# Hybrid attention/mLSTM layer on one core: the second feed-forward's gated tiles turned by VectorE and a trip through DRAM instead of TensorE, its down products taken by pairs of column blocks

## The chip, the core and the metric

The kernel runs on one core of a Trainium2 chip. A core has five engines that each work through a queue of their own, in order: PE (TensorE, matrix products), DVE (VectorE), ACT (ScalarE), POOL (GpSimd) and SP (SyncE, which here only issues transfers). They wait for each other by semaphores. Sixteen DMA engines move data between DRAM and the core's memory SBUF; a transfer is issued by SP, ACT or POOL and lands some time later. Products are summed in PSUM, used here as eight banks of 128 x 512 float32.

The metric is device time of one execution in microseconds, the median of several runs; lower is better.

## The reference

One layer of a diffusion backbone on 256 latent tokens and 256 context tokens of width 2048, all float32: a half-step SwiGLU feed-forward, a mixing stage (grouped-query attention beside a bidirectional mLSTM), and a second half-step SwiGLU feed-forward. The change is in the second feed-forward, which only the 256 latent tokens pass through:

```python
def half_step_ffn(x, mod, i, g, w_up, w_down):
    h = adaln(x, g, mod, i)
    a, b = jnp.split(h @ w_up, 2, axis=-1)
    return x + 0.5 * mod[:, i + 2, None, :] * ((jax.nn.silu(a) * b) @ w_down)
```

`D_FF` is 5632. A "gated tile" below is a piece of `silu(a) * b`: 128 tokens by 512 hidden columns.

## The kernel before, in words

**Products in three parts.** A float32 operand is split into a high part `hi` (rounded to the format float32r) and the rest `lo`. `split` (L120) does this for each half of a loaded weight tile of 128 x 2048: ACT writes `hi`, DVE writes `lo`, 128 x 1024 each, into rings of four buffers. `mm3` (L148) then issues three matmuls: high by high, and the two mixed ones. So for each megabyte of weights ACT and DVE make two passes each, and PE issues 12 matmuls (quads, below) or 24 (up and down steps).

**Hidden blocks.** The 5632 hidden columns are 11 blocks of 512, `n` = 0 to 10. Block 0 is made together with the end of the mixing stage, block 10 by plain up steps (`up`, L2180). Blocks 1 to 9 are made by `quad(n)` (L2078): the tokens are two halves `t` of 128, the 2048 inputs two halves, and seven products of combinations of those quarters (Strassen's scheme in Winograd's form) take the place of eight. Its seven products, `m` = 0 to 6, are two steps `s` each, one for each weight tile `q`. Their weights are sums of slices of `w_up2b`, made while they load: POOL's `accum` transfers (L740, a helper's line) add a slice to a buffer `chain` or `ra` that already holds one; SP loads the plain ones (`raw`, `ra`, `chain`). `summed_half` adds two buffers on DVE. At the end of `m` = 4 the gated tile of `t` = 0 exists (`c12`), at the end of `m` = 6 that of `t` = 1 (`c21`), each as 128 tokens (partitions) x 512 hidden columns, in a tile `ca`, with the sign reversed.

**Turning.** The down product needs the hidden columns on the partitions. `turned` (L2044) does it: four PE transposes of 128 x 128 into one PSUM bank (L2058), then ACT writes the high half `hid2h` from PSUM (L2061, which also mends the sign) and DVE the low half `hid2l` (L2063). It is called after every step; a tile is turned two steps after it was made (`N_TURN`). Block 10's two tiles (`sab`) go the same way.

**Down steps.** `down(n0, n1)` (L2213) multiplies two hidden blocks by their slices of `w_dn2`, for the four blocks of 512 output columns in turn: (n0, column 0), (n1, column 0), (n0, column 1) and so on, one step `u` each, a megabyte of `w_dn2` and 24 matmuls. After the second step of a column the two sums are added to `acc2` (L2229 on DVE, L2227 on ACT the first time). `units` strings the up steps of block 10 and down(0,1), (2,3), (4,5), (6,7); down(8,9) follows the last quad, and `last2` (L2278) does block 10 and the final norm.

**Order.** `sequence` (L2242) sets it: `s s` for each of the seven products, with a `u` after m = 1, 2, 4 and 5 (after all of 1 to 6 in the first quad). A scheduler then orders each engine's queue by its own estimate of times; only instructions marked `pinned` keep their order in the program. The first feed-forward already turns its tiles by the other way: `nc.vector.transpose` (L840), stores by SP to `hidd` (L842), loads by SP (`hid_load`, L705), and halves by `split_to` (L716, instructions at L720 and L721).

Of the kernel before, what the change touches and what calls it, by code (L numbers as in the profile page):

```python
# [37 lines left out]
N_TURN = 2  # L38
# [20 lines left out]
def tile_layer(ctx: ExitStack, tc: tile.TileContext, I: dict, out: bass.AP):  # L59
# [1871 lines left out]
    with f2x:  # L1931
# [111 lines left out]

        def turned():  # L2044

            if not turn:
                return
            n, t, sa, sign = turn[0]
            if clock[0] < born[n, t] + N_TURN:
                return  # L2050
            if n not in hids:
                if n - 1 not in hids or len(hids) - len(summed) >= N_HID:
                    return
                hids[n] = hid_tiles()
            turn.pop(0)
            tb = tbank()
            for j in range(FB):
                nc.tensor.transpose(tb[:, j * P : (j + 1) * P], sa[:, j * P : (j + 1) * P], ident)  # L2058
            t3 = tb.rearrange("p (j c) -> p j c", j=FB)
            hh, hl = (x[:, :, t * P : (t + 1) * P] for x in hids[n])  # L2060
            nc.scalar.activation(hh, t3, AF.Copy, scale=sign)  # L2061
            if sign < 0:
                nc.vector.scalar_tensor_tensor(hl, t3, -1.0, hh.bitcast(F32), op0=ALU.mult, op1=ALU.subtract)  # L2063
            else:
                nc.vector.tensor_tensor(hl, t3, hh.bitcast(F32), op=ALU.subtract)
            done.add((n, t))
# [3 lines left out]
        def wait_turn(n, t, sa, sign):  # L2070
            turn.append((n, t, sa, sign))
            born[n, t] = clock[0]
            turn.sort(key=lambda x: x[:2])

        def ca_tile():
            return f2b.tile([P, CB], F32, tag="ca", name="ca", bufs=3)

        def quad(n):  # L2078

            add = lambda o, x, y: nc.vector.tensor_tensor(o, x, y, op=ALU.add)  # L2080
            mul = lambda o, x, y: nc.vector.tensor_tensor(o, x, y, op=ALU.mult)
# [18 lines left out]
            def c12():  # L2100
                add(g["b"], B["X"], g["b"])
                mul(g["a"], g["a"], g["b"])
                wait_turn(n, 0, g["a"], -1.0)
# [76 lines left out]
        def up(n):  # L2180

            sab = []
            for ab in range(2):
                bs = [bank() for _ in range(2)]
                for u in range(4):
# [7 lines left out]
                    if u == 3:  # L2193
                        for t in range(2):
                            if ab:
                                nc.vector.tensor_tensor(sab[t], sab[t], bs[t], op=ALU.mult)
                                wait_turn(n, t, sab[t], 1.0)
# [15 lines left out]
        def down(*ns):  # L2213

            for cb in range(NCB):
                c = slice(cb * CB, (cb + 1) * CB)
                bs = [bank() for _ in range(2)]
                for n in ns:
                    assert (n, 1) in done or not n
                    wt = load_split(I["w_dn2"][n, cb])  # L2220
                    for t in range(2):
                        block(bs[t], n, wt, t, n == ns[0], n == ns[-1])
                    if n == ns[-1]:
                        for t in range(2):
                            a = acc2[:, t, c]
                            if not ns[0]:
                                nc.scalar.activation(a, bs[t], AF.Copy)  # L2227
                            else:
                                nc.vector.tensor_tensor(a, a, bs[t], op=ALU.add)  # L2229
                            if n == LAST - 1:  # L2230
                                half_gated(a, a, late["g8"][:, c])
                                accum(a, x2d[t * P : (t + 1) * P, c])
                        if cb == NCB - 1:
                            summed.update(ns)
                    yield
# [40 lines left out]
        drain(down(LAST - 2, LAST - 1))  # L2276
# [72 lines left out]
def _laid_out(a):  # L2349
# [30 lines left out]
    for n in "12":  # L2380
# [14 lines left out]
        rows = dn.reshape(NF // FB, FB, P, NCB, CB).transpose(0, 3, 2, 1, 4).reshape(NF // FB, NCB, P, 2048)  # L2395
        if n == "1":
            turned = dn.reshape(NF // FB, 4, FB, 32, NCB, CB).transpose(0, 4, 1, 3, 2, 5).reshape(NF // FB, NCB, P, 2048)
            rows = np.concatenate([rows[:1], turned[1:]])
        m[f"w_dn{n}"] = asc(rows)
# [34 lines left out]
```

## Time and profile before

| what | value |
|---|---|
| median of 3 runs | 2594.59 us (2590.64 to 2597.07) |
| the profiled execution | 2588.91 us, of which the span from the first to the last instruction is 2587.2 us |
| granted TensorE clock, mean | 0.995 |
| PE busy | 2555.3 us, 99% of the span |
| DVE busy | 2206.6 us, 85% |
| ACT busy | 1405.5 us, 54% |
| POOL busy | 221.9 us, 9% |
| moved by DMA | 684.70 MB, mean 265 GB/s |
| L2058, the transposes of `ca` | 72, first at 2000.3 us, last at 2514.6 us |
| weight transfers of a megabyte in the second feed-forward, issue to landing | medians 8.7 to 11.4 us |

In the rows, L152 is the line of `mm3`, so all products are there and are told apart by the tiles: `mm<-hi,hid2h` is a down step, `X<-` and `Y<-` are quads. L128 and L129 are the two instructions of `split`. Matmuls overlap each other in the pipeline: the time that one takes of PE is the distance between two starts, not its shown length. "DMA share" is the mean busy share of the sixteen engines.

### The profile page before, as it was taken

The page shows a single profiled execution, that of the slowest core. Times are in us where ns is not written, and L with a number is a line of the kernel's source. Part 1 is how long each engine was busy: PE and PEld are TensorE (multiplying, and loading weights), DVE is VectorE, ACT ScalarE, POOL GpSimd, SP SyncE. Part 2 cuts the span into 40 slices and gives each one's busy share as a digit, 9 for nine tenths or more (in the row PEclk, how much of TensorE's full clock was granted, in tenths as well). Part 3 has the DMA queues.
Part 4 walks back from the last instruction along what each step waited for, and adds up shares of the span by engine and source line. Part 5 has one row for each costly group of instructions (what it writes and reads, how often), then busy time and mean ns, then how long its engine had stood idle before and what let it go on. Part 6 is the DMA issues. An engine that isn't in the chain of part 4 may idle for free. (4 is left out here: it accounts for less than half of the span.)

```text
span 2587.2 us, 33868 instructions
## 1 busy us (share of the span) xinstructions
PE 2555.3 (99%) x12486; PEld 2124.7 (82%) x12486; DVE 2206.6 (85%) x2924; ACT 1405.5 (54%) x1798; POOL 221.9 (9%) x271
## 2 busy tenths in 40 slices
PE   8999999999999999999999999999999999999998
PEld 5788888888887878888889889888898888888886
DVE  7789888888888788888887888898889888898987
ACT  5454444444444455444454347466486676667763
POOL 0000000100010100010110000120000000000001
PEclk8999999999999999999999999999999999999999
DMA  9989999999999999999987897776768999999985
GB/s 392 355 214 275 265 290 277 262 292 281 276 285 282 255 236 246 213 221 231 231 242 268 295 315 242 237 282 212 267 233 246 275 277 283 278 286 278 273 248 171
DMA packets 153478, 684.70 MB, mean 265 GB/s; under 512 B 22872, under 2 KB 43864, under 8 KB 92000
## 3 DMA queue, kind: packets, MB, share of 16 engines
q1 hardware_dynamic: 123936, 490.64, 51.7%
q0 software_dynamic: 29376, 191.90, 37.3%
q8 instruction: 98, 1.61, 0.2%
q14 instruction: 68, 0.56, 0.1%
HBM read 664.59 MB, written 17.89 MB: 264 GB/s over the span
## 5 line engine op out<-in xcount | busy, mean ns | idle before, releaser
L128 ACT ACTIVATE hi<-raw 128x1024 fp32r<-128x1024 f32 (+2 forms) x488 | 504.5, 1040 | 401.2 <-PE mm L152 298.7
L129 DVE TENSOR_TENSOR lo<-raw,hi 128x1024 fp32r<-128x1024 f32 (+2 forms) x476 | 567.2, 1204 | 105.7 <-ACT hi L128 87.4
L128 ACT ACTIVATE hi<-chain 128x1024 fp32r<-128x1024 f32 x352 | 370.1, 1059 | 352.6 <-PE mm L152 199.3
L129 DVE TENSOR_TENSOR lo<-chain,hi 128x1024 fp32r<-128x1024 f32 x352 | 425.2, 1219 | 92.5 <-ACT hi L128 81.2
L152 PE MATMUL mm<-hi,hhi 128*128 128x512 f32 (+3 forms) x1024 | 390.7, 382 | 0.0
L152 PE MATMUL mm<-lo,hhi 128*128 128x512 f32 (+3 forms) x1024 | 387.7, 379 | 1.9 <-DVE lo L129 1.8
L152 PE MATMUL mm<-hi,hlo 128*128 128x512 f32 (+3 forms) x1024 | 386.6, 378 | 0.0
L208 DVE SCALAR_TENSOR_TENSOR junk<-sraw,cBh 128x1024 fp8e5<-128x1024 f32 x192 | 234.3, 1220 | 40.5 <-DMA sraw<-in_w_mt 39.0
L152 PEld LDWEIGHTS mm<-lo,hhi 128*128 128x128 f32 x1024 | 192.8, 188 | 37.0 <-DVE lo L129 4.0
L152 PEld LDWEIGHTS mm<-hi,hlo 128*128 128x128 f32 x1024 | 193.0, 189 | 32.0
L152 PEld LDWEIGHTS mm<-hi,hhi 128*128 128x128 f32 x1024 | 192.9, 188 | 32.2 <-ACT hi L128 0.3
L129 DVE TENSOR_TENSOR lo<-ra,hi 128x1024 fp32r<-128x1024 f32 x104 | 126.2, 1222 | 25.6 <-ACT hi L128 21.7
L128 ACT ACTIVATE hi<-ra 128x1024 fp32r<-128x1024 f32 x104 | 110.1, 1062 | 64.0 <-PE mm L152 34.2
L152 PE MATMUL mm<-lo,hid2h 128*128 128x512 f32 x352 | 137.1, 389 | 0.0
L152 PE MATMUL mm<-hi,hid2h 128*128 128x512 f32 x352 | 137.1, 389 | 0.0
L152 PE MATMUL mm<-hi,hid2l 128*128 128x512 f32 x352 | 137.0, 389 | 0.0
L152 PE MATMUL mm<-hi,sumshl 128*128 128x512 f32 x400 | 123.2, 389 | 0.0
L208 DVE SCALAR_TENSOR_TENSOR sr<-sr,cBl 128x1024 f32<-128x1024 f32 x84 | 102.1, 1222 | 16.4 <-DMA sr<-in_w_mt 15.1
L740 POOL DMA_DIRECT2D chain<-in_w_up1b x60 | 53.1, 886 | 724.1 <-DVE lo L129 583.9
L152 PE MATMUL mm<-hi,sumshh 128*128 128x512 f32 x352 | 108.3, 389 | 0.0
L152 PE MATMUL mm<-hhi,hi 128*128 128x512 f32 (+1 forms) x288 | 101.4, 352 | 0.0
L152 PE MATMUL mm<-hhi,lo 128*128 128x512 f32 (+1 forms) x288 | 99.0, 344 | 0.0
(490 smaller groups left out, 5415.1 us busy)
## 6 DMA issues: line engine op xcount, KB each, us to landing
raw<-in_w_dn SPq DMA_DIRECT2D x70, 1024.0 KB, 10.0
chain<-in_w_up1b POOLq DMA_DIRECT2D x60, 1024.0 KB, 10.7
sraw<-in_w_mt SPq DMA_DIRECT2D x96, 512.0 KB, 8.4
sr<-in_w_mt SPq DMA_DIRECT2D x81, 512.0 KB, 5.7
raw<-in_w_up1b SPq DMA_DIRECT2D x40, 1024.0 KB, 9.1
mraw<-in_w_m SPq DMA_DIRECT2D x32, 1024.0 KB, 7.6
chain<-in_w_dn POOLq DMA_DIRECT2D x30, 1024.0 KB, 10.2
chain<-in_w_up2b POOLq DMA_DIRECT2D x28, 1024.0 KB, 11.4
```

Of the source, the lines that this page charges most:

```text
L128: scalar[0].activation(hi, src, AF.Copy)
L129: vector[0].tensor_tensor(lo, src, hi.bitcast(F32), op=ALU.subtract)
L152: tensor[0].matmul(out_ap, s, m, start=first and not n, stop=last and n == 2, skip_group_check=skip)
L208: ins = nc.vector.scalar_tensor_tensor(junk() if junk else raw, raw, 1.0, cB[s], op0=ALU.mult, op1=ALU.mult, accum_out=mT[:, i, s, kt, h : ...
L740: accum = lambda dst, src: nc.gpsimd.dma_start(dst, src, accum_op=ALU.add)
```

## The change

- A quad's gated tile is now made with its right sign (`negative`, a scalar_tensor_tensor in place of a tensor_tensor). One step later DVE's transpose exchanges rows and columns inside each 32 x 32 square, from `ca` into the tile of the second factor (`spare`: `ca` or `cy`).
- At set places counted in steps, ACT's queue issues the rest: after 1 step (`N_STORE`) a store of the 128 x 512 tile to a DRAM tile `hid2`, after 4 and 5 steps (`N_FETCH`) two loads each of a band of 32 partitions, as 32 x 4 runs of 128 elements, and after 8 steps (`N_MOVE`) the high half (ACT) and low half (DVE), now from SBUF. All of these are pinned. A load waits for its tile's store to have landed.
- The rows of `w_dn2` for blocks 1 to 9 are laid out on the host in the order that this gives the hidden columns.
- Block 10's tiles still go through PE. The two PSUM banks of the transposes join the four for products.
- `down` takes column blocks in pairs: (n0, 0), (n0, 1), (n1, 0), (n1, 1), then the same for 2 and 3. At the end, the store and the loads of the last tile are placed around the first two steps of down(8,9), and block 10's transposes come after those.

```diff
-N_TURN = 2
+N_TURN = 1
+N_STORE = 1
+N_FETCH = 4
+N_MOVE = 8
...
-        ps["mm"] = ctx.enter_context(pool(name="ps2", bufs=4, space=PSUM))
+        ps["mm"] = ctx.enter_context(pool(name="ps2", bufs=6, space=PSUM))
         psx = ctx.enter_context(pool(name="psx", bufs=1, space=PSUM))
-        ps["tr"] = ctx.enter_context(pool(name="pt2", bufs=2, space=PSUM))
...
+        def halves(n, t, x, runs=False):
+            hh, hl = (y[:, :, t * P : (t + 1) * P] for y in hids[n])
+            if runs:
+                hh, hl = (y.rearrange("p j (a c) -> p a j c", c=32) for y in (hh, hl))
+            pinned(nc.scalar.activation(hh, x, AF.Copy))
+            pinned(nc.vector.tensor_tensor(hl, x, hh.bitcast(F32), op=ALU.subtract))
+            done.add((n, t))
+
         def turned():
...
-            tb = tbank()
-            for j in range(FB):
-                nc.tensor.transpose(tb[:, j * P : (j + 1) * P], sa[:, j * P : (j + 1) * P], ident)
-            t3 = tb.rearrange("p (j c) -> p j c", j=FB)
-            hh, hl = (x[:, :, t * P : (t + 1) * P] for x in hids[n])
-            nc.scalar.activation(hh, t3, AF.Copy, scale=sign)
-            if sign < 0:
-                nc.vector.scalar_tensor_tensor(hl, t3, -1.0, hh.bitcast(F32), op0=ALU.mult, op1=ALU.subtract)
...
+            if spare is not None:
+                turn.pop(0)
+                nc.vector.transpose(spare, sa)
+                moved.append((clock[0], n, t, sa, spare))
...
+        def stored(n, t, sa, spare):
+            pinned(nc.scalar.dma_start(hid2d[n][t], spare))
+
+        def fetched(n, t, sa, spare, bands):
+            rows = hid2d[n][t].rearrange("(a r) (b x) -> b r a x", a=4, b=4)
+            for b in bands:
+                pinned(nc.scalar.dma_start(sa[32 * b : 32 * b + 32].rearrange("r (a x) -> r a x", a=4), rows[b]))
+
+        def arrived():
+
+            for then, *x in moved:
+                age = clock[0] - then
+                if age == N_STORE:
+                    stored(*x)
+                elif age in (N_FETCH, N_FETCH + 1):
+                    b = 2 * (age - N_FETCH)
+                    fetched(*x, (b, b + 1))
+            if moved and clock[0] >= moved[0][0] + N_MOVE and room(moved[0][1]):
+                _, n, t, sa, _ = moved.pop(0)
+                halves(n, t, sa.rearrange("p (a j c) -> p a j c", a=4, j=FB), True)
...
-                mul(g["a"], g["a"], g["y"])
-                wait_turn(n, 1, g["a"], -1.0)
+                negative(g["a"], g["y"])
+                wait_turn(n, 1, g["a"], g["y"])
...
-            for cb in range(NCB):
-                c = slice(cb * CB, (cb + 1) * CB)
-                bs = [bank() for _ in range(2)]
+            for c0 in (0, 2):
+                bs = {}
                 for n in ns:
...
+                    for cb in (c0, c0 + 1):
...
-        while turn:
-            clock[0] += 1
-            turned()
-        before_final()
-        drain(down(LAST - 2, LAST - 1))
+        before_final()
+        final = down(LAST - 2, LAST - 1)
+        for gap, more in ((N_STORE, True), (N_FETCH - N_STORE, False), (1, True)):
+            clock[0] += gap
+            arrived()
+            if more:
+                next(final)
+        while moved:
+            clock[0] += N_MOVE
+            arrived()
+        while turn:
+            turned()
+        drain(final)
```

How the queues stand now. The first place is on ACT where quad 4 has ended and quad 5 runs its products m = 1 and m = 2 (`chain` and `ra` are the two pairs of weight buffers, `raw` the plain loads; `ca<-ca` is a silu, `ca<-X` a copy from PSUM). Before:

```order
L128 ACTIVATE hi<-raw 128x1024
L2112 ACTIVATE ca<-ca 128x512
L128 ACTIVATE hi<-raw 128x1024 x2
L2061 ACTIVATE hid2h<-tr 128x4x128
L128 ACTIVATE hi<-raw 128x1024
L2086 ACTIVATE ca<-X 128x512
L128 ACTIVATE hi<-raw 128x1024 x2
L128 ACTIVATE hi<-chain_15897 128x1024 x2
L2090 ACTIVATE ca<-ca 128x512
L128 ACTIVATE hi<-chain_15898 128x1024 x2
```

and with the change:

```order
L134 ACTIVATE hi<-raw 128x1024
L2151 ACTIVATE ca<-ca 128x512
L134 ACTIVATE hi<-raw 128x1024 x3
L2087 DMA hid_15907<-cy 128x512
L2125 ACTIVATE ca<-X 128x512
L2064 ACTIVATE hid2h<-ca 128x4x4x32
L134 ACTIVATE hi<-raw 128x1024 x2
L2092 DMA ca<-hid_15907 32x4x128 x2
L134 ACTIVATE hi<-chain_15894 128x1024
L2129 ACTIVATE ca<-ca 128x512
L2092 DMA ca<-hid_15907 32x4x128 x2
L134 ACTIVATE hi<-chain_15894 128x1024
```

Between the store (L2087) and the first pair of loads (L2092) ACT has a copy, the halves of the other tile and two weight passes; behind each pair stands a weight pass of product m = 2.

The second place is on DVE a little later, from the last pass over the first weight tile of m = 2 to the first `ra` tile of m = 3 (the rows `chain<-chain,ra` are `summed_half`; `raw` is m = 2's down step). Before:

```order
L129 TENSOR_TENSOR lo<-chain_15897,hi 128x1024
L2080 TENSOR_TENSOR chain_15897<-chain_15897,ra_15899 128x1024 x2
L129 TENSOR_TENSOR lo<-chain_15898,hi 128x1024
L2080 TENSOR_TENSOR chain_15898<-chain_15898,ra_15900 128x1024
L129 TENSOR_TENSOR lo<-chain_15898,hi 128x1024
L129 TENSOR_TENSOR lo<-raw,hi 128x1024 x2
L129 TENSOR_TENSOR lo<-ra_15899,hi 128x1024 x2
```

and with the change:

```order
L2119 TENSOR_TENSOR chain_15894<-chain_15894,ra_15896 128x1024
L135 TENSOR_TENSOR lo<-chain_15894,hi 128x1024
L135 TENSOR_TENSOR lo<-chain_15895,hi 128x1024 x2
L135 TENSOR_TENSOR lo<-raw,hi 128x1024 x2
L2065 TENSOR_TENSOR hid2l<-ca,hid2h 128x4x4x32
L2119 TENSOR_TENSOR chain_15894<-chain_15894,ra_15896 128x1024
L135 TENSOR_TENSOR lo<-ra_15896,hi 128x1024 x2
```

The addition that stood between the two passes over `chain_15898` stands elsewhere now; the two passes over the same tile, here `chain_15895`, follow each other.

The third place is the end on ACT with the change, after the silu of the last quad's last tile (here `raw` are tiles of `w_dn2`, and `hid2h<-mm` are block 10's halves):

```order
L134 ACTIVATE hi<-raw 128x1024 x4
L2151 ACTIVATE ca<-ca 128x512
L2087 DMA hid_15912<-cy 128x512
L134 ACTIVATE hi<-raw 128x1024 x2
L2092 DMA ca<-hid_15912 32x4x128 x2
L2064 ACTIVATE hid2h<-ca 128x4x4x32
L2092 DMA ca<-hid_15912 32x4x128 x2
L134 ACTIVATE hi<-raw 128x1024 x2
L2064 ACTIVATE hid2h<-ca 128x4x4x32
L2064 ACTIVATE hid2h<-mm 128x4x128 x2
```

Before, the last tile's four transposes stood on PE 15 matmuls into the down steps; now its halves (the second `hid2h<-ca`) come behind the store, both pairs of loads and four weight passes.

More of the change, by code (lines that the diff above doesn't have):

```diff
@@ L2042, in tile_layer, with room @@
         born, clock = {}, [0]
+        hid2d = {n: dr.tile([2, P, CB], F32, name=f"hid2{n}") for n in QUADS}
+        moved = []
+        def room(n):
+            if n not in hids:
+                if n - 1 not in hids or len(hids) - len(summed) >= N_HID:
+                    return False
+                hids[n] = hid_tiles()
+            return True
+        def halves(n, t, x, runs=False):
[5 more added lines that the diff above has]
+            done.add((n, t))
         def turned():
@@ L2059, in turned @@
-            t3 = tb.rearrange("p (j c) -> p j c", j=FB)
-            hh, hl = (x[:, :, t * P : (t + 1) * P] for x in hids[n])
-            nc.scalar.activation(hh, t3, AF.Copy, scale=sign)
-            if sign < 0:
[L2063 to L2066, printed above, removed]
+            if spare is not None:
+                turn.pop(0)
+                nc.vector.transpose(spare, sa)
+                moved.append((clock[0], n, t, sa, spare))
+            elif room(n):
+                turn.pop(0)
+                tb = bank()
+                for j in range(FB):
+                    nc.tensor.transpose(tb[:, j * P : (j + 1) * P], sa[:, j * P : (j + 1) * P], ident)
+                halves(n, t, tb.rearrange("p (j c) -> p j c", j=FB))
```

61 lines of the change are left out of this document (31 added, 30 removed).

## The prediction

> **What bounds the kernel now.** I read the busy time by stretches first, then the chain of waits, then the list of waits, all for the stretch from 2000 to 2500 us, in which the quads' tiles are turned (columns of the first: PE, weight load, DVE, ACT and POOL busy with their counts, granted clock, DMA share, GB/s).
>
> ```profile
> 2000.00:2100.00 100.00, 100.00 (x450) 82.66 (x449) 84.42 (x80) 69.87 (x76) 6.98 (x8) 1.00 0.96 292
> 2200.00:2300.00 100.00, 99.47 (x445) 81.81 (x444) 91.03 (x88) 69.29 (x74) 8.84 (x11) 1.00 0.92 274
> sum 500.00, PE 499.46 PEld 412.21 DVE 438.35 ACT 347.15 POOL 41.89; mean PE 99.89 PEld 82.44 DVE 87.67 ACT 69.43 POOL 8.38
> ```
>
> PE is busy for 499.5 of 500 us at full clock: it is the bound, and each PE instruction that goes is time that goes, as long as nothing else becomes late. The chain agrees (start, length, what):
>
> ```profile
> 2427.32 5.45 PE mm L152 x24
> 2432.76 0.44 PE tr L2058 x4
> 2433.20 5.45 PE X L152 x24
> ```
>
> The transposes are a link of it. But the cover is thin elsewhere (total us, times, longest):
>
> ```profile
> ACT hi L128 <- DMA chain<-in_w_up2b: 18.1, 7, 3.9
> ACT hi L128 <- DMA ra<-in_w_up2b: 9.7, 4, 2.8
> PE Y L152 <- DVE lo L129: 0.5, 1, 0.5
> ```
>
> Eleven times ACT waits for a weight that is still under way, up to 3.9 us; once this reaches PE. So DMA is not the bound on average, but there are places with almost nothing to spare.
>
> **What goes: PE.** The start times of PE's rows around one group of four transposes:
>
> ```profile
> 2504.18 0.39 PE L152 MATMUL mm<-lo,hid2h 128*128 128x512 f32 x1
> 2504.42 0.60 PE L2058 MATMUL tr<-ident,ca 128*128 128x128 f32 x4
> 2504.77 0.48 PE L152 MATMUL Y<-hi,h2hi 128*128 128x512 f32 x1
> 2505.09 0.40 PE L152 MATMUL Y<-hi,h2lo 128*128 128x512 f32 x1
> 2505.32 0.40 PE L152 MATMUL Y<-lo,h2hi 128*128 128x512 f32 x1
> ...
> L2058 PE MATMUL tr<-ident,ca x72: 270/272/304, 2000.3 to 2514.6; 128*128 128x128 f32 x72
> ```
>
> Products start every 0.23 us. From 2504.18 to 2505.09 two of them take 0.91 us, so the group costs 0.91 - 0.46 = 0.45 us, far less than four times its shown 0.27 us. 72 transposes are 18 groups: 18 x 0.45 = 8.1 us. Block 10's two groups stay.
>
> **What is added on DVE and ACT.**
>
> ```profile
> L840 DVE STREAM_TRANSPOSE c<-ca x20: 691/704/711, 208.3 to 922.5; 128x512 f32<-128x512 f32 x20
> L845 DVE SCALAR_TENSOR_TENSOR ca<-ca,cy x20: 679/684/693, 232.7 to 929.8; 128x512 f32<-128x512 f32 x20
> L2063 DVE SCALAR_TENSOR_TENSOR hid2l<-tr,hid2h x18: 683/684/694, 2002.6 to 2515.5; 128x512 fp32r<-128x512 f32 x18
> L721 DVE TENSOR_TENSOR sumshh<-hidl,sumshh x9: 1217/1219/1222, 944.3 to 1204.6; 128x1024 fp32r<-128x1024 f32 x9
> L842 SPq DMA_DIRECT2D hid<-c x20: 326/327/1792, 209.1 to 923.2; - x20
> L711 SPq DMA_DIRECT2D hidh<-hid x20: 325/480/704, 949.0 to 1229.8; - x20
> ```
>
> The first feed-forward shows the same instructions. The new one is the transpose, 0.70 us; the halves from SBUF in runs of 32 cost no more than those from PSUM (1.22 us for 1024 columns against 0.68 for 512), nor does the signed product (0.68 us; the plain product L2081 takes 0.68, in a row below). DVE gets 18 x 0.70 = 12.6 us into 500 - 438 = 62 idle ones: nothing, with PE as cover; were DVE the bound it would be 12.6 us. ACT gets five issues a tile, by SP's rows 0.33 + 4 x 0.48 = 2.3 us, 41 us into 153 idle ones: nothing as a sum. The danger is the order, because ACT's weight passes stand behind these issues.
>
> **ACT behind the store.** The first pair of loads waits until the store has landed, and product m = 2's weight passes wait behind it. Quad 4's second tile, from ACT's timeline and PE's (a pass of ACT is 1.06 us):
>
> ```profile
> 2211.02 1.06 ACT L128 ACTIVATE hi<-raw 128x1024 fp32r<-128x1024 f32 x1
> 2218.07 0.63 ACT L2090 ACTIVATE ca<-ca 128x512 f32<-128x512 f32 x1 [0.54 <-DVE ca L2080]
> 2222.41 2.01 ACT L128 ACTIVATE hi<-chain 128x1024 fp32r<-128x1024 f32 x2 [3.70 <-DMA chain<-in_w_up2b]
> 2221.95 0.62 PE L152 MATMUL Y<-hi,n1f 128*128 128x512 f32 x2
> ```
>
> The store can go at 2212.1 and lands L later. Behind it come a pair of loads (1.0), a pass (1.06), the silu (0.63), a pair (1.0), a pass (1.06) and its DVE pass (1.22): 6.0 us, so the second half of m = 2's first weight tile is ready at 2218.1 + L. PE starts m = 2 at 2221.95 and takes that low half as its ninth matmul, at 2223.8. An L up to 5.6 us costs nothing; beyond that each microsecond costs one, eight times over (quads 2 to 9 each follow such a tile). A first tile's store (t = 0) goes out one pass sooner, and its second pair stands behind both passes; by the same count it pays only from about 7.5 us. L has no row on ACT's queue, so I bound it:
>
> ```profile
> hid<-c SPq DMA_DIRECT2D x20, 256.0 KB, 7.4
> x2d<-x SPq DMA_DIRECT2D x8, 256.0 KB, 4.5
> out<-acc SPq DMA_DIRECT2D x8, 256.0 KB, 2.9
> ```
>
> These are stores of the same 256 KB: 2.9 us with the engines nearly free, 7.4 in the first feed-forward's full traffic, but behind megabyte loads in SP's own queue. ACT's queue holds nothing else, so I take 4.5 us: cost 0. At 7.4 it is 8 x 1.8 = 14 us.
>
> The Trainium skill ("DMA: Bandwidth & Descriptors", section "Anatomy of one DMA") gives a transfer about 2.0 us plus its bytes at 436 GB/s, by estimate 2.6 us for this store. The quiet row of 2.9 us agrees, the 7.4 us in traffic don't; by the rule this step costs 0 as well.
>
> **Weights that come later.** Per tile 0.26 MB are stored and 0.26 MB loaded on the same 16 engines.
>
> ```profile
> 2208.00:2212.00 4.00, 4.00 (x21) 3.15 (x20) 4.00 (x5) 3.58 (x5) 0.87 (x1) 1.00 0.97 205
> 2220.00:2224.00 4.00, 4.00 (x20) 3.30 (x19) 1.95 (x3) 1.59 (x2) 0.00 (x0) 1.00 1.01 418
> 2224.00:2228.00 4.00, 3.47 (x16) 2.56 (x15) 3.97 (x4) 3.26 (x4) 0.00 (x0) 1.00 0.37 156
> ...
> 2223.50 1.23 DVE L129 TENSOR_TENSOR lo<-chain,hi 128x1024 fp32r<-128x1024 f32 x1 [2.06 <-PE Y L152]
> 2224.76 1.22 DVE L2080 TENSOR_TENSOR chain<-chain,ra 128x1024 f32<-128x1024 f32 x1
> 2225.90 1.22 DVE L129 TENSOR_TENSOR lo<-chain,hi 128x1024 fp32r<-128x1024 f32 x1
> ```
>
> From 2208 to 2224 the engines are full, at 205 GB/s while accumulating and 418 with plain loads; then comes a gap (share 0.37). The waiting weight of 2222.41 lands at the end of the full stretch, and the store and first pair of a second tile (0.39 MB) now fall into it: 0.9 us later at 418 GB/s, 1.9 at 205. PE also arrives 0.45 us sooner. Against that, the addition between the two DVE passes (2224.76) now stands elsewhere, as the order rows show. It made the second pass end at 2227.1, and this is PE's one stall of 0.5 us, which goes. Without it the first pass decides: it ends at 2224.7, and PE, 12 matmuls after 2221.95, takes that low half as its third, at 2225.1. That is 0.4 us to spare, so a wait of about 3.7 + 0.4 = 4.1 us would be hidden. I apply that to all eleven places, of which these are the longest but the 3.70, and the shortest:
>
> ```profile
> 2012.30 2.01 ACT L128 ACTIVATE hi<-chain 128x1024 fp32r<-128x1024 f32 x2 [3.85 <-DMA chain<-in_w_up2b]
> 2465.96 2.01 ACT L128 ACTIVATE hi<-chain 128x1024 fp32r<-128x1024 f32 x2 [3.00 <-DMA chain<-in_w_up2b]
> 2283.09 2.01 ACT L128 ACTIVATE hi<-ra 128x1024 fp32r<-128x1024 f32 x2 [2.75 <-DMA ra<-in_w_up2b]
> 2137.07 1.06 ACT L128 ACTIVATE hi<-chain 128x1024 fp32r<-128x1024 f32 x1 [0.64 <-DMA chain<-in_w_up2b]
> ```
>
> At 0.9 + 0.45 = 1.35 us later only the waits of 3.85, 3.70 and 3.00 run over: 1.1 + 0.95 + 0.25 = 2.3 us. At 1.9 + 0.45 = 2.35 whatever exceeds 1.75 does, which is all but the shortest: 27.8 - 0.64 - 10 x 1.75 = 9.7 us. The new traffic is plain, so I take 2.3.
>
> **The end.** The last tile has only two down steps as cover.
>
> ```profile
> 2511.01 3.40 PE mm L152 x15
> 2513.41 0.68 DVE L2081 TENSOR_TENSOR ca<-ca,cy 128x512 f32<-128x512 f32 x1
> ```
>
> It is gated at 2514.1 and transposed at 2514.8. With L = 4.5 the first pair goes out by 2520.3, the other tile's halves and the second pair by 2521.9; the loads land 4.5 us later at 2526.4, and the high half is there at 2527.0. PE's two steps (10.9 us from 2511.0), block 10's transposes (0.9) and the first tile's 12 matmuls (2.7) end at 2525.5: 1.5 us of stall. With 2.9 us for both transfers it is 0; with L = 7.4 it is 4.4.
>
> **Sum.** -8.1 - 0.5 + 0 + 2.3 + 1.5 = -4.8 us. The profiled execution took 2588.9 us (span 2587.2, and 1.7 around it), so it would take 2584.1. The median of the runs shown lies 5.7 above the profiled execution: 2589.8.
>
> **Rivals.**
> - *Nothing comes late.* The stores land in 2.9 us and the gaps take the traffic: -8.6 us, 2586.0. For it: the first feed-forward does the same at a DMA share near 1. Against: its steps are twice as long, and SP, not ACT, waits there.
> - *ACT stands behind the store* (slower). L is 7.4 us as for `hid<-c`: -8.6 + 14 + 2.3 + 4.4 = +12.1, 2606.7. It decides from L = 5.6 on, cancels the gain at 6.1 us and passes it from there. For it: the same shape in the same traffic took 7.4. Against: that was behind SP's own loads. The Trainium skill (same page, "Issuing engines are not separate DMA queues") says that transfers of all issuers interleave on the same engines and a second issuer saves issue time alone; by this rule ACT's queue would help little, and the time is this rival's. No row of ACT's queue can tell.
> - *The weights come later by the slow rate.* -8.6 + 9.7 + 1.5 = +2.6: 2597.2. For it: the waiting weights are the accumulated ones, and their stretch begins at 205 GB/s. Against: what is added takes the engines' time by the plain rate.
>
> **How the numbers follow.** Forecast 0.40, nothing late 0.25, ACT behind the store 0.20, late weights 0.15. 0.3%, about what a measurement of this kernel can tell from no change, is 7.8 us: faster means below 2586.8. Most of "nothing late" lies there and a little of the forecast: 0.27. Slower means above 2602.4: ACT behind the store for the most part and the tail of late weights: 0.21. Within: 0.52. The forecast's own range is 2586 to 2594; with the others, 2584 (nothing late, and 2 us of scatter) to 2606.
>
> **What would show it.** No L2058 groups on `ca`, and 24 matmuls in 5.45 us without a gap: the gain. The store's median landing below or above 5.6 us, and ACT waiting for `hid` by name: which of forecast and second rival. Waits of ACT for `chain` and `ra` grown from 27.8 us in total, with PE rows released by `lo`: late weights. DVE above 95% in a stretch, or PE stalls where none of the three stands, would make the prediction wrong.

## The result and the profile after

The changed kernel takes 2669.81 us, median of 4 runs (2667.53 to 2672.66), against 2593.30 us of the kernel before in runs beside it (2590.64 to 2597.07): 76.5 us more, a ratio of 1.030 (95% interval 1.0285 to 1.0315). The prediction was 2589.8 us with a range of 2584 to 2606. It was wrong in size and in sign. The profiled execution took 2670.43 us (span 2668.7).

The busy time by stretches, after (columns as in the prediction; the lines of the code have moved: the passes are L134 and L135, the products L158, the store L2087, the loads L2092, the halves L2064 and L2065):

```profile
2000.00:2100.00 100.00, 95.91 (x410) 77.20 (x409) 77.97 (x77) 62.66 (x69) 6.98 (x8) 0.98 0.95 284
2200.00:2300.00 100.00, 88.78 (x371) 71.03 (x370) 73.28 (x74) 54.98 (x60) 6.99 (x8) 0.96 0.90 257
```

```profile
2000.00:2500.00 500.00, 458.35 (x1902) 365.99 (x1901) 387.09 (x379) 295.04 (x322) 36.64 (x42) 0.96 0.89 256
```

PE was busy for 499.5 of these 500 us before and is now for 458.4, at a granted clock of 0.96 instead of 1.00. What it waits for stands in the list of waits, after, 2000 to 2500 us (total us, times, longest):

```profile
ACT hi L134 <- DMA hid<-cy: 54.5, 6, 9.7
PEld Y L158 <- ACT hi L134: 40.5, 13, 5.2
ACT hi L134 <- DMA hid<-ca: 35.8, 4, 9.1
PE Y L158 <- ACT hi L134: 35.1, 12, 4.8
ACT ca L2147 <- DMA hid<-ca: 5.2, 1, 5.2
```

ACT waits 95.5 us for stores, and PE behind it. The eleven waits for `chain` and `ra` of before (27.8 us) are all gone: ACT is late for another reason when it gets there. One place, ACT's timeline after quad 4's second tile:

```profile
2240.43 0.34 ACTq L2087 DMA_DIRECT2D hid<-cy  x1
2240.82 0.60 ACT L2125 ACTIVATE ca<-X 128x512 f32<-128x512 f32 x1 [0.39 <-PE Y L158]
2241.31 0.62 ACT L2064 ACTIVATE hid2h<-ca 128x512 fp32r<-128x512 f32 x1
2241.84 2.00 ACT L134 ACTIVATE hi<-raw 128x1024 fp32r<-128x1024 f32 x2
2252.32 0.80 ACTq L2092 DMA_DIRECT2D ca<-hid  x2
2253.24 1.06 ACT L134 ACTIVATE hi<-chain 128x1024 fp32r<-128x1024 f32 x1 [9.41 <-DMA hid<-cy]
```

and the chain of waits of the same kernel there (start, length, what):

```profile
2240.43 11.88 DMA hid<-cy
...
2253.24 1.07 ACT hi L134
2254.31 0.02 issue
2254.33 1.24 DVE lo L135
2255.57 0.04 issue
2255.61 6.41 PE Y L158 x22
```

The store needs 11.88 us; ACT has 3.2 us of work before the loads that wait for it. Over all stores (the view by line, after):

```profile
DMA to landing us min/median/max: 4.9/11.9/12.9
```

The smallest is the last store, at the end: no accumulating load runs beside its pieces, and the engines are busy for 0.55 of the time that these take. So the prediction's second rival came, with a landing far above its bound of 7.4 us. But the experiments show a second loss behind it.

### The profile page after: what moved, and what is told of

The parts are those of the page before. It is cut to its first block, busy times and chain, and to the rows that moved or that the text cites. A ratio compares the mean times of both kernels' runs of the same rounds, so it can differ in the third digit from the quotient of the medians.

```text
span 2668.7 us, 33880 instructions
## 1 busy us (share of the span) xinstructions
PE 2579.4 (97%) x12414; PEld 2126.4 (80%) x12414; DVE 2209.9 (83%) x2942; ACT 1395.1 (52%) x1798; POOL 221.7 (8%) x271
## 4 chain that ended last, share of the span: by engine, by line
PE 28%; DMA 11%; DVE 7%; issue 2%; ACT 1%; ACTq 1%; POOL 0%; SPq 0%; POOLq 0%; DVEq 0%
PE mm L158 16%; PE Y L158 5%; DMA hid<-ca 4%; DMA hid<-cy 4%; PE X L158 3%; DVE lo L135 3%; DVE sr L214 1%; DMA sr<-in_w_mt 1%; ACT hi L134 1%; ACTq L2092 1%; DVE early L214 1%; DVE cy L1421 0%; PE tr L158 0%; DMA raw<-in_w_mk 0%; DMA ra<-in_w_up2b 0%
## 5 line engine op out<-in xcount | busy, mean ns | idle before, releaser
L134 ACT ACTIVATE hi<-raw 128x1024 fp32r<-128x1024 f32 (+2 forms) x488 | 502.6, 1039 | 402.0 <-PE mm L158 282.0
L135 DVE TENSOR_TENSOR lo<-raw,hi 128x1024 fp32r<-128x1024 f32 (+2 forms) x476 | 564.9, 1201 | 105.7 <-ACT hi L134 88.5
L134 ACT ACTIVATE hi<-chain 128x1024 fp32r<-128x1024 f32 x352 | 367.9, 1058 | 393.8 <-PE mm L158 206.6
L135 DVE TENSOR_TENSOR lo<-chain,hi 128x1024 fp32r<-128x1024 f32 x352 | 422.2, 1218 | 129.0 <-ACT hi L134 125.2
L158 PE MATMUL mm<-hi,hhi 128*128 128x512 f32 (+3 forms) x1024 | 390.0, 381 | 0.0
L158 PE MATMUL mm<-lo,hhi 128*128 128x512 f32 (+3 forms) x1024 | 387.0, 378 | 2.7 <-DVE lo L135 2.7
L158 PE MATMUL mm<-hi,hlo 128*128 128x512 f32 (+3 forms) x1024 | 386.1, 377 | 0.0
L158 PEld LDWEIGHTS mm<-lo,hhi 128*128 128x128 f32 x1024 | 192.4, 188 | 37.9 <-DVE lo L135 5.2
L158 PEld LDWEIGHTS mm<-hi,hhi 128*128 128x128 f32 x1024 | 192.5, 188 | 32.1 <-ACT hi L134 0.4
L158 PEld LDWEIGHTS mm<-hi,hlo 128*128 128x128 f32 x1024 | 192.6, 188 | 32.0
L135 DVE TENSOR_TENSOR lo<-ra,hi 128x1024 fp32r<-128x1024 f32 x104 | 124.0, 1219 | 56.2 <-ACT hi L134 54.3
L134 ACT ACTIVATE hi<-ra 128x1024 fp32r<-128x1024 f32 x104 | 108.2, 1058 | 97.9 <-PE mm L158 31.1
L158 PE MATMUL mm<-hi,hid2h 128*128 128x512 f32 x352 | 137.2, 390 | 1.9 <-ACT hid2h L2064 1.9
L158 PE MATMUL mm<-hi,hid2l 128*128 128x512 f32 x352 | 137.2, 390 | 0.5 <-DVE hid2l L2065 0.5
L158 PE MATMUL mm<-lo,hid2h 128*128 128x512 f32 x352 | 137.2, 390 | 0.0
L158 PE MATMUL mm<-hi,sumshl 128*128 128x512 f32 x400 | 123.2, 389 | 0.0
L158 PE MATMUL mm<-hi,sumshh 128*128 128x512 f32 x352 | 109.2, 392 | 0.0
L158 PE MATMUL mm<-hhi,hi 128*128 128x512 f32 (+1 forms) x288 | 101.4, 352 | 0.0
L158 PE MATMUL mm<-hhi,lo 128*128 128x512 f32 (+1 forms) x288 | 99.0, 344 | 0.0
```

Of the source, the lines that this page charges most:

```text
L134: scalar[0].activation(hi, src, AF.Copy)
L135: vector[0].tensor_tensor(lo, src, hi.bitcast(F32), op=ALU.subtract)
L158: tensor[0].matmul(out_ap, s, m, start=first and not n, stop=last and n == 2, skip_group_check=skip)
```

## A quad's time as a yardstick

From ACT's first copy of a quad (product m = 0) to the same copy six quads later, kernel before and then after:

```profile
2090.30:2456.20 365.90, 365.36 (x1633) 301.54 (x1632) 324.06 (x309) 254.09 (x269) 31.41 (x36) 1.00 0.95 276
```

```profile
2100.30:2526.10 425.80, 385.44 (x1591) 306.63 (x1590) 327.42 (x322) 246.79 (x268) 31.40 (x36) 0.96 0.88 253
```

A quad lasts 61.0 us before and 71.0 after. Before, that is PE's own time: seven products and four down steps, 24 matmuls or 5.45 us each, and two groups of transposes of 0.45, 60.9. But the row's DMA share of 0.95 says as well that the sixteen engines are busy for some 58 us of each quad and idle for 3. The trip's own share is in the page after, as ACT's queue (packets, MB, share of the sixteen engines over the span):

```profile
q10 hardware_dynamic: 12960, 9.44, 1.1%
```

1.1% of 2668.7 us is 29 us in nine quads, 3.3 a quad: about all that was idle. The same table for every run, with DMA time summed from the trace's records of single pieces over six quads (us a quad; the median, and its distance from the median of the kernel before that ran beside it, in us; distances below are taken between the numbers of this last column):

```
run            a quad  DMA busy  DMA idle   median   less before
before           61.0      57.7       3.3
pe_pairs         61.2      57.6       3.6   2592.1          +2.5
noturn           62.0      57.3       4.7   2596.3          +4.7
notrip           62.2      57.9       4.3   2595.5          +3.9
storeonly        62.6      58.9       3.7   2597.0          +5.4
loadonly         63.9      59.8       4.1   2610.8         +19.3
nowait           65.9      61.6       4.3   2624.0         +34.4
placed           64.4      61.0       3.4   2623.2         +31.6
fetch6           70.6      61.2       9.3   2663.8         +74.2
after            71.0      62.6       8.4   2669.8         +76.5
small            75.7      62.6      13.1   2706.6        +117.0
light_before     61.0      56.3       4.7   2592.7          +1.2
light_notrip     60.3      55.7       4.7   2584.0          -7.6
light_nowait     64.2      59.6       4.6   2611.7         +20.1
```

## The experiments

**First round: is it the wait, the traffic or the order?** Three theories stood: W, ACT standing behind the store; T, the added transfers themselves; O, the column pairs, six banks and the new order of the queues.

*nowait*, the loads without their dependence:

```diff
-            rows = hid2d[n][t].rearrange("(a r) (b x) -> b r a x", a=4, b=4)
+            rows = I["w_dn2"][n, 0, :, t * CB : (t + 1) * CB].rearrange("(a r) (b x) -> b r a x", a=4, b=4)
```

> The changed kernel, but the loads read a slice of w_dn2 of the same shape instead of the stored tile, so the second feed-forward's gated values are wrong; the stores, the loads and their places stay, only the dependence of load on store is gone. Theory W (the loss is ACT standing behind the store): the waits of ACT for hid (about 113 us in all) are gone, PE is busy again for about 99.5 of 100 us and the granted clock goes back to 1.00 there: 2583 to 2595 us. Theory T (the added transfers themselves delay the weights): still above 2640 us, with ACT waiting for chain, ra and raw. Theory O (column pairs, six banks and the scheduler's new order cost it): still above 2640 us.

Measured: 2624.0 us (2621.8 to 2626.1), ratio 1.0125 (1.0108 to 1.0142). Neither W's number nor T's: 42 us less than the changed kernel, 34 us more than the one before. ACT's waits for `hid` are gone, but the weights are late now. Waits of this kernel, 2000 to 2500 us:

```profile
ACT hi L134 <- DMA ra<-in_w_up2b: 31.8, 9, 5.4
ACT hi L134 <- DMA chain<-in_w_up2b: 24.8, 9, 5.5
ACT hid2h L2064 <- DMA ca<-in_w_dn: 19.5, 9, 4.8
```

56.6 us for `chain` and `ra` instead of 27.8. So there are two losses, and W is somewhat over half.

*pe_pairs*, the trip undone alone (beside the edit: `w_dn2` laid out as before, `N_TURN = 2`):

```diff
-                wait_turn(n, 0, g["a"], g["b"])
+                wait_turn(n, 0, g["a"], None)
...
-                wait_turn(n, 1, g["a"], g["y"])
+                wait_turn(n, 1, g["a"], None)
```

> The changed kernel with the trip undone alone: all tiles turned by PE's transposes two steps after their birth as before, w_dn2 laid out as before; column pairs, six banks, the sign in the product and four ca buffers stay. W and T: the 18 groups of 0.45 us are back and nothing else is lost: 2588 to 2600 us. O: above 2640 us.

Measured: 2592.1 us, ratio 1.0003 (0.9992 to 1.0013): no difference. O falls: column pairs, banks, the signed product and a fourth `ca` buffer, which the change also brings, cost nothing. The order that the queues have with the trip isn't in this run; *notrip*, below, has nearly the same.

*fetch6*, the loads two steps later:

```diff
-N_FETCH = 4
+N_FETCH = 6
-N_MOVE = 8
+N_MOVE = 10
```

> The changed kernel with the loads two steps later (N_FETCH 6, N_MOVE 10), all else the same. In ACT's queue three or more pairs of weight passes then stand between a store and its first load instead of two. W: two more steps are 10.9 us of PE, and a store lands after 12 to 13 us against the some 4 us that were covered, so the waits for hid fall from 113 us to under 15 us: 2584 to 2600 us. T or O: 2655 to 2675 us, as the number and the size of the transfers and the order of products are unchanged.

Measured: 2663.8 us (ratio 1.0280, 1.0263 to 1.0298). A miss: 2 us came back where W expected some 70. The chain of waits of this kernel shows why, and its timeline of ACT what follows:

```profile
2169.93 18.69 DMA hid<-cy
...
2188.64 0.31 ACTq L2092
```

```profile
2169.93 0.34 ACTq L2087 DMA_DIRECT2D hid<-cy  x1
...
2188.99 0.63 ACT L2129 ACTIVATE ca<-ca 128x512 f32<-128x512 f32 x1 [10.65 <-DMA hid<-cy]
```

Two steps later, the second pair of a first tile's loads stands straight ahead of the second tile's store in ACT's queue (at 2166.3 and 2166.7, the store at 2169.9). By the records of pieces the store's first piece moves 11.8 us after its issue, where it moved after 3.8 us in the changed kernel: it goes behind its own queue's 256 small pieces. The store lands after 18.7 us instead of 11.9, and ACT still waits 10.65 us. The two steps also gave less cover than the 10.9 us that I had put on them: ACT is through with the passes in between at 2178.3, 8.4 us after the store's issue, so that a landing after 11.9 us would have been late as well. This says nothing against W, only that the place was bad.

*small*, the stored rows cut in two, to see what makes a landing:

```diff
-        hid2d = {n: dr.tile([2, P, CB], F32, name=f"hid2{n}") for n in QUADS}
+        hid2d = {n: dr.tile([2, 2, P, CB // 2], F32, name=f"hid2{n}") for n in QUADS}
...
-            pinned(nc.scalar.dma_start(hid2d[n][t], spare))
+            pinned(nc.scalar.dma_start(hid2d[n][t].rearrange("h p x -> p h x"), spare.rearrange("p (h x) -> p h x", h=2)))
...
-            rows = hid2d[n][t].rearrange("(a r) (b x) -> b r a x", a=4, b=4)
+            rows = [hid2d[n][t][b // 2][:, b % 2 * P : b % 2 * P + P].rearrange("(a r) x -> r a x", a=4) for b in range(4)]
```

> The changed kernel with each stored row of 2048 B cut in two in DRAM, so that a store is 256 pieces of 1024 B instead of 128 of 2048 B, the same bytes, places and number of instructions; the loads read the same values. Theory R (each of the 16 engines takes one piece from each active queue in turn, so that a store of 8 pieces an engine takes about 4 us to start and 8 rounds of 0.31 + 0.63 + 0.08 us): 16 rounds of about 1.0 us, the landing goes from 11.9 to about 20 us median, the waits of ACT grow by some 8 us at 17 places, and the time by 90 to 140 us: 2760 to 2810 us. Theory B (the bytes, or a fixed delay of a loaded system, set the landing): 11.5 to 13 us and 2660 to 2685 us.

Measured: the landing has a median of 14.2 us (4.6 to 15.9), the time is 2706.6 us (ratio 1.0438, 1.0418 to 1.0457), 40 more than the changed kernel. Same bytes and longer, so theory B falls; but R expected about 20 us and at least 90 us more. The records of pieces tell what is right in R. For the store at 2240.43 of the changed kernel, when every sixteenth of its 128 pieces starts, from the ninth on (us after the issue):

```
4.97  6.07  7.10  8.11  9.12  9.52  9.88  10.04
```

After some 4 us come waves of 16 pieces, as many as there are engines, 1.0 us apart: the time of one accumulated piece (0.63), one plain one (0.31) and one of its own (0.08). The turns can be read from the starts: a piece of SP's at 6.67, one of ACT's at 6.99, one of POOL's at 7.07, the next of SP's at 7.67. (The records name the queue of a piece, not its engine.) From 9.12 on POOL's transfer is through, and the waves are 0.4 us apart or less. The profile's view of transfers of that stretch, 2244 to 2252, has the sums for SP (q1), POOL (q0) and ACT (q10), packets first:

```profile
q1 hardware_dynamic: 216, 1.64, 50.1%
q0 software_dynamic: 98, 0.67, 42.6%
q10 hardware_dynamic: 144, 0.26, 8.5%
```

In *small* there are 16 waves, but POOL's queue had few pieces to set against 256 (median 80, at most 130), so most waves are short ones: from a store's first piece to its last start 9.8 us pass instead of 7.1 (medians without the last store). R is right in kind, and its size depends on how long the other queues have work.

**Second round: what does the traffic cost?** *notrip* leaves out stores and loads, *storeonly* and *loadonly* put one of the two back (*loadonly* with the source of *nowait*):

```diff
             for then, *x in moved:
                 age = clock[0] - then
-                if age == N_STORE:
-                    stored(*x)
-                elif age in (N_FETCH, N_FETCH + 1):
-                    b = 2 * (age - N_FETCH)
-                    fetched(*x, (b, b + 1))
```

> The changed kernel without stores and loads: the halves are taken from the gated tile as it stands, not exchanged, so the second feed-forward's output is wrong; VectorE's transposes, the halves from SBUF in runs of 32, the column pairs and the six banks stay. If everything but the transfers costs nothing, only the 8 us of PE's transposes are gone: 2580 to 2586 us, against a kernel before of 2590. If VectorE's 12.6 us more or the halves' form cost something: 2590 or more.

> As notrip, but the 18 stores are there again and nothing reads them (output wrong in the same way). Theory T2 (the 16 DMA engines are full in this stretch, their busy share was 0.92 to 0.98 before, so what the added pieces take of them is paid): a store is 128 pieces of 0.084 us, 0.67 us of each engine, 18 of them 12 us: 8 to 14 us above notrip. Theory Q (what costs is ACT's queue: loads late behind the store and ACT waiting for them): as notrip within 3 us.

> As notrip, but the 72 loads are there at their places, from a slice of w_dn2 that nothing writes (the gated values are wrong), without stores. T2: a tile's loads are 512 pieces of 512 B, 0.03 to 0.04 us each, some 1.2 us of each engine, 18 of them 20 to 24 us, and 15 to 26 us above notrip; with storeonly's part this adds up to the 34 us that the run with both but no dependence lay above the kernel before, and the 8 us. Theory Q: the loads no longer stand behind a store, land in under 8 us instead of 13, and the time is within 8 us of notrip.

Measured: 2595.5 us for *notrip* (ratio 1.0015, 1.0003 to 1.0027), 2597.0 for *storeonly* (1.0014, 1.0003 to 1.0026), 2610.8 for *loadonly* (1.0074, 1.0052 to 1.0097). The surprise is *notrip*: the four transposes a tile are gone, nothing is added but VectorE's work, and the 8 us don't appear. PE is earlier, and the weights are late without any added transfer. Waits of this kernel, 2000 to 2500 us, where the kernel before had 18.1 and 9.7:

```profile
ACT hi L134 <- DMA chain<-in_w_up2b: 28.8, 10, 4.8
ACT hi L134 <- DMA ra<-in_w_up2b: 21.3, 8, 3.9
```

The store alone costs 1.5 us, which can't be told from nothing, not the 8 to 14 of T2; the loads alone cost 15.4 us, at T2's lower end, and both together 30.5: more than the sum. A quad's DMA time grows by 1.0, 1.9 and 3.7 us, and the quad by 0.4, 1.7 and 3.7. The first microsecond is largely absorbed; with both, all 3.7 are paid.

**Third round: what takes the 8 us in notrip?** Either VectorE's 1.4 us a quad (D), or the weights' transfers as a second bound just behind PE (M). *noturn* leaves out VectorE's transposes too; *light_notrip* and *light_nowait* make one of a quad's six accumulating loads a plain one:

```diff
-                nc.vector.transpose(spare, sa)
```

```diff
-                    accum(ra[1], part(n, 1, 1))
+                    nc.gpsimd.dma_start(ra[1], part(n, 1, 1))
```

> As notrip, and VectorE's 18 transposes left out too (the halves are taken from the gated tile, output wrong in the same way). What is left of the change is PE without 16 of its 18 groups of transposes' time on quads, the halves from SBUF, column pairs and six banks. A quad lasted 60.9 us before and 62.2 in notrip, where PE alone would need 59.9. Theory D (VectorE's 1.4 us a quad or its new order made notrip slow): 60.0 us a quad, 2578 to 2585 us. Theory M (the weights' transfers are a second bound just behind PE: the DMA engines are busy 57.7 us of a quad and some 3.3 us of each stay idle between stretches, so that a quad can't go below about 61 us): 60.7 to 61.5 us a quad, 2587 to 2594 us.

> As notrip, but one of the six accumulating loads of each quad (the second addition to ra[1]) is a plain load of the same megabyte on the same queue, so that one product's weights are wrong as well. 128 pieces at 0.31 instead of 0.63 us take 2.6 us a quad off each DMA engine. Theory M: the weights no longer bind, a quad falls from 62.2 to 59.9 to 60.4 us and the 8 us of PE appear: 2574 to 2584 us. Theory D: as notrip, 2592 to 2599 us.

> The run with stores and loads but no dependence between them, with the same lighter load as in light_notrip. M: 65.9 - 2.6 = 63.3 us a quad, 18 to 27 us less than that run's 2624: 2597 to 2606 us. If instead ACT's queue (late loads, halves waiting) set its time: 2618 us or more.

Measured: *noturn* 2596.3 us (1.0018, 1.0004 to 1.0032), as *notrip* and 2 us above M's range: D falls. *light_notrip* 2584.0 us (0.9974, 0.9963 to 0.9986), at the edge of M's range, 11.5 us less than *notrip* and 7.6 less than the kernel before. Six quads of *notrip* and of *light_notrip*:

```profile
2090.70:2463.90 373.20, 366.95 (x1586) 294.78 (x1585) 326.47 (x319) 246.91 (x270) 31.33 (x36) 1.00 0.93 270
```

```profile
2091.40:2453.30 361.90, 360.94 (x1586) 296.77 (x1585) 329.11 (x321) 250.69 (x270) 29.32 (x36) 1.00 0.92 279
```

PE, idle for 6.3 us of the first stretch, is busy again for 360.9 of 361.9 us. The queues of PE, VectorE and ScalarE are the same in both, row by row. *light_nowait* 2611.7 us (1.0077, 1.0061 to 1.0093): 14.3 less than *nowait*, where M gave 18 to 27. A quad lost 1.7 us, its DMA time 2.0 (not the 2.6 that I had worked out). M holds in direction, and about two thirds of its number; ACT's waits for the loads (19.5 us in *nowait*) are still there, and no run takes them out with the transfers left in.

The lighter load shortens the engines' work and the landings together: in the stretches above, SP's loads of `ra`, which the edit doesn't touch, land after a median of 9.7 us instead of 12.0. So these runs show that the weights' transfers hold PE up. They don't separate full engines from the round of buffer, load and pass behind them, in which POOL's next load waits until VectorE has passed over the buffer's last one (in *notrip*, 2000 to 2500 us, POOL waits 234.7 us for this before its loads to `ra`).

*light_before*, the same lighter load in the kernel before, as the fourth corner:

> The kernel before, with the lighter load alone (one of six accumulating loads of each quad plain, one product's weights wrong). Before, a quad took 60.9 us, of which PE needs 60.9, and the DMA engines' 57.7 us and 3.3 idle come to the same. If PE binds before the change (as predicted): 2588 to 2594 us, no change, and the distance to light_notrip (2584) is the 8 us of PE's transposes. If the transfers were already ahead of PE: 2580 to 2586 us.

Measured: 2592.7 us (1.0009, 1.0000 to 1.0018): no gain, though its DMA engines idle for 4.7 us a quad now. So PE does bind before; without its transposes and with lighter transfers the same program takes 2592.7 - 2584.0 = 8.7 us less. The kernel before stood on two bounds at once, and taking work off either one alone yielded nothing.

**Last: places where ACT doesn't stand.** *placed* keeps the whole computation and puts all four loads of a first tile 5 steps after its transpose and of a second tile 8 steps after, behind no other load:

```diff
-N_FETCH = 4
+N_FETCH = 5, 8
-N_MOVE = 8
+N_MOVE = 10, 12
...
-                elif age in (N_FETCH, N_FETCH + 1):
-                    b = 2 * (age - N_FETCH)
-                    fetched(*x, (b, b + 1))
+                elif age == N_FETCH[x[1]]:
+                    fetched(*x, range(4))
```

> The changed kernel with its computation whole and only the places changed: all four loads of a quad's first tile 5 steps after its transpose, of the second 8 steps after (three more than now and behind no other load), halves after 10 and 12 steps. W (about 45 of the 76 us are ACT standing behind the store): the waits of ACT for hid fall under 15 us and the time comes to that of the run without dependence: 2615 to 2632 us. M says that it can't come under about 2610 us, since the DMA engines' 61.5 us a quad and 4 us of gaps remain. If the waits only move elsewhere, as they did with the loads two steps later: above 2645 us.

Measured: 2623.2 us (2621.9 to 2623.7), ratio 1.0120 (1.0101 to 1.0139): 45 us of the loss are back by the place alone, and it meets *nowait*. Its six quads and its largest wait of ACT for a store, 2000 to 2500 us:

```profile
2093.90:2480.20 386.30, 370.31 (x1584) 299.70 (x1583) 327.57 (x320) 247.96 (x269) 31.40 (x36) 0.98 0.95 277
```

```profile
ACT ca L2146 <- DMA hid<-ca: 36.3, 6, 7.6
```

I had expected under 15 us of such waits. The first tiles' loads still stand up to 7.6 us, but at 5 steps most of this is hidden. What is left fits the transfers' bound: 61.0 us of DMA time and 3.4 idle a quad, about the idle time of before the change. It isn't taken apart further; part of the 36.3 us of waits may be in it.

## Why the prediction was wrong, step by step

- **What bounds the kernel now.** PE is the bound, as said (*light_before* against *light_notrip*). The false step is the one after it, that each PE instruction that goes is time that goes, and that "DMA is not the bound on average". Its condition, that nothing else becomes late, failed by the gain itself: in *notrip* PE was earlier, nothing was moved, and the weights were late. The quoted rows had the hint: shares of 0.96 and 0.92 mean 2.4 to 4.9 idle us in 61. The runs in which PE had to wait for weights left no less (3.4 to 4.7 of DMA idle in *notrip*, *noturn*, *storeonly*, *loadonly*, *nowait* and *placed*), so an idle time of 3.3 was nothing to spare. That PE at 60.9 us and the transfers at 57.7 + 3.3 come to the same proves nothing by itself, since busy and idle time always make up the quad; that the two were level is shown by *light_before*, *notrip* and *light_notrip*.
- **What goes: PE, -8.1 us.** The size is right: 8.7 us with lighter loads, and the second of *notrip*'s quads, measured between ACT's copies, lasts 59.8 us against 60.8 (the later ones 61.2 to 63.7). Over the whole of *notrip* nothing of it is left.
- **What is added on DVE and ACT: nothing.** Right for VectorE: the transposes take 0.70 us, as predicted, and *noturn* without them is no faster than *notrip*. ACT's five issues a tile were not taken out without their transfers.
- **ACT behind the store: 0.** The mechanism was described as it came; the term that was mis-sized is L. I took 4.5 us and bounded it at 7.4; it is 11.9. The bound failed because `hid<-c` was a store of the same size in another mix of queues. By the records of pieces at most one of POOL's ran beside any of those twenty stores; the pieces of 18 of them started within 1.5 to 3.6 us of the first, and the rest of their 7.4 us was mostly the wait for the first piece. A landing in traffic was no property of the bytes here: 4 us, then eight waves whose length is one piece of every queue that has work. The trace of before had this case too: two of the first feed-forward's stores `hid<-cy`, beside 129 and 139 of POOL's pieces, took 6.1 and 6.4 us from first to last. The durations of such pieces were in the trace of before (0.63 accumulated, 0.31 plain): with the 3.8 us that a start took in the changed kernel, 3.8 + 8 x 1.02 = 12.0 us. With L = 11.9 the prediction's own count gives 59.9 + (11.9 - 5.6) + (11.9 - 7.5) = 70.6 us a quad, near the measured 71.0; in part by luck, since PE idles only 6.7 us of a quad (425.8 - 385.4 over six) and takes 4.1 longer for the same products than in *light_notrip* (385.4 against 360.9). The granted clock of 0.96 instead of 1.00 would make some 3 of these.
- **Weights that come later: +2.3 (bounds 2.3 to 9.7).** Far too small: in *notrip*, without any traffic, the 8 us were gone and 4 more, and *nowait* and *placed* lie another 30.5 and 27.7 us above it. I asked at eleven waiting places how much later a transfer would land. The right question was the whole quad: 3.3 us more of DMA time in a loop that had 3.3 idle. That the waits for `chain` and `ra` vanished in the changed kernel hid this, since ACT came later than the weights; my sign for late weights read "no", while the transfers cost some 30 us in the two runs that have them all and in which ACT stood less. The sign did read "yes" in *notrip*, with 50.1 us against 27.8.
- **The end: +1.5 (0 to 4.4).** Right: 2.4 us. The waits of PE after 2590 us, after:

```profile
PE mm L158 <- ACT hid2h L2064: 1.9, 2, 1.5
PE mm L158 <- DVE hid2l L2065: 0.5, 2, 0.2
```

  The last store landed in 4.9 us and the last load in 4.5, where I had put 4.5 for both.
- **Rivals.** The slower one with chance 0.20 named the place and the price per microsecond. The Trainium skill's rule that stood beside it ("DMA: Bandwidth & Descriptors", "Issuing engines are not separate DMA queues") agrees with the trace: the store's pieces take turns with SP's and POOL's (the starts at 6.67, 6.99, 7.07 and 7.67 above). The same page's figure for a transfer, which it fitted to transfers that GpSimd issues, gives by estimate 2.6 us for this store; from ACT's queue 11.9 us was measured in traffic and 4.9 at the end.

The two losses don't simply add: 45 us of standing and some 30 of traffic are what comes off when standing is taken away first. While ACT stands, weights' buffers aren't freed, and the DMA engines catch up (idle 8.4 us a quad in the changed kernel). That this is why is argued, not shown. Open is also why *notrip* idles 1 us a quad more than before (4.3 against 3.3 of DMA, and 62.2 us against 61.0) though it has less to do; *noturn* rules out VectorE's transposes, and no run separates the halves' place from the queues' new order.

No version that computes the whole layer beats the kernel before: *placed*, the best with the trip, is 31.6 us slower, and *pe_pairs* no different.

## What to carry to other kernels

Compare each engine's busy time over one period of the loop with the period, the DMA engines among them. Where two of them were level, as here, taking work off one yielded nothing, and what was moved to the other was paid for: of 1.0 us of DMA time a quad little, of 3.7 us all. Bound a transfer's landing in traffic by the time to its first piece (some 4 us here) and pieces per engine times one piece of every queue that is then at work, not by its bytes or by a store in another stage. A load that waits for a store doesn't belong on an engine that has weights to pass behind it, unless the store's landing, and whatever stands ahead of it in its own queue, is covered by passes in between.

## What the runs showed of the hardware

- The DMA engines took single pieces from the queues in turn: a store's 128 pieces of 2048 B of ACT's queue, 8 an engine, all started within 7.1 us (median) beside pieces of 8192 B at 0.63 (accumulating) and 0.31 us (plain), and within 1.5 us at the end, with none of POOL's beside them. In the changed kernel first pieces moved 3.6 to 4.8 us after the issue in traffic and 2.8 us at the end; in *fetch6*, behind 256 pieces of their own queue, after 11.5 to 12.8.
- A stall cost more than its length. After the stall at 2252 the changed kernel's granted clock falls (the same columns as above):

```profile
2240.00:2252.00 12.00, 10.43 (x47) 8.29 (x45) 6.11 (x7) 3.44 (x5) 0.00 (x0) 1.00 0.98 277
2252.00:2258.00 6.00, 3.38 (x8) 2.12 (x8) 3.64 (x4) 4.76 (x6) 0.00 (x0) 0.72 0.72 281
2258.00:2264.00 6.00, 6.00 (x28) 4.99 (x27) 6.00 (x6) 4.69 (x6) 0.00 (x0) 0.99 0.17 30
```

The 22 products behind it took 6.41 us instead of 22 x 0.227 = 5.0. The Trainium skill ("TensorE: Matmul & The Clock Gate", "What's actually happening") says that the slow clock is the state at rest and that activity lifts it; the rows agree, with 0.72 in the 6 us around the stall's end and 0.99 in the next 6.
